# When the second weight-sum buffer of a gate/up pair is claimed: with the other three, or where it is first written

## The chip, the core and the metric

The kernel runs on one core of a Trainium2 chip. The core has a matrix engine (PE, with its weight loads as PEld), a vector engine (DVE), a scalar engine (ACT), a general engine (POOL) and a queue that issues transfers (SP). Each works through its own list of instructions in order and waits on semaphores of the others. The metric is the time of one execution in microseconds (us), as the median of several runs. A profiled execution gives the trace, in which times count from the first instruction.

## The reference

One layer of a hybrid block: a mixer of four parts, a cross attention over a memory, and a feed-forward part, each followed by a layer norm. The change lies in the feed-forward part:

```python
D_MODEL = 1024; SEQ = 1024; D_FF = 2816

def swiglu_ffn(x, w_gate, w_up, w_down):
    return (jax.nn.silu(x @ w_gate) * (x @ w_up)) @ w_down
...
        h = swiglu_ffn(x, w_ff_gate[l], w_ff_up[l], w_ff_down[l])
        x = layer_norm(DEEPNORM_ALPHA * x + h, ln_ff_g[l], ln_ff_b[l])
```

All arrays are float32.

## The kernel before

The 2816 columns of the gate and up weights are cut into 22 tiles of 128, taken two at a time: 11 pairs (`NPAIR`). For each pair the 2x2 blocks of weights and of x are multiplied by a scheme with seven block products in place of eight, so sums and differences of weight blocks are needed. A product is 24 matmuls of 128x512: two halves of the output (m = 0, 1), four blocks of depth, and three matmuls each, since every operand is split in a high and a low part (`whi`, `wlo`; `split`, L149 on ACT and L150 on DVE).

`gu_stream` (L622 to L658) makes the weights of the products, pair after pair, as a generator that is asked for a product two ahead of PE. For a pair it loads four tiles of 128x1024: `r11` and `r12` into `wraw` buffers, `r21` and `r22` into `gr` buffers (L627). POOL then makes s1 = r21 + r22, s2 = s1 - r11, r21 = r11 - r21 and r12 = r12 - s2 (all L631). s1 and s2 stand in two `gs` buffers, the last sum is written over the `wraw` of r12. The seven weights are used in the order r11, r12, s1, s2, r12', r21', r22.

`gu_first` runs the products of r11 and r12 into the banks `gc`; after the first, ACT copies the two halves of the bank to a buffer `ge` (L679), and the second accumulates into the same banks, so its halves wait for those copies. `gu_rest` runs the other five into `gb`, `ga`, `gb`, `ga`, `ga`; DVE takes the halves out (L694), and POOL makes four more sums of the results (L694), which SP stores (`hA`, `hS`, L713). From the third pair on, `down_sums` (L604 to L612) has POOL prepare one pair of rows of the down weights: two loads into `dw` buffers (L608), four differences (L611), four stores (`tT`, L612). The later down stage reads `hS` and `tT` again.

The 128x1024 buffers all come from one pool of 37, `c4`, and a scheduler that simulates the program decides at build time which freed buffer a claim gets, and how the instructions stand on each engine. A claim writes two columns on POOL at once, and is held in the order of all other claims, so that it waits on POOL until the buffer's last reader is done:

```python
    def big(self, s, dt=F32):
        t = self.c4.tile([P, 1024], dt, tag="c4", name=self.nm(s))
        i = self.nc.gpsimd.memset(t[:, 0:2].bitcast(F32), 0.0)
        if self.touch is not None:
            self.order(i, self.touch)
```

In the profile these claims are the MEMSET rows of L136. A load into a claimed buffer follows its claim.

Of the kernel before, what the change touches and what calls it, by code (L numbers as in the profile page):

```python
# [37 lines left out]
class Kernel:  # L38
# [583 lines left out]
    def gu_stream(self):  # L622
        nc, g = self.nc, self.nc.gpsimd
        wt = lambda: self.wp.tile([P, WCH], F32, tag="wraw", name=self.nm("wraw"), bufs=3)

        def load(t, i, q):
            nc.sync.dma_start(t, self.a["w_gu"][i, q])  # L627
            return t

        def sub(o, x, y, op=ALU.subtract):  # L630
            g.tensor_tensor(out=o, in0=x, in1=y, op=op)  # L631

        for i in range(NFIRST):
            for q in range(2):
                yield self.versions(load(wt(), i, q))
        for i in range(NPAIR):
            r11 = load(wt(), i, 0)
            if i >= NFIRST:
                yield self.versions(r11)
            r12 = load(wt(), i, 1)  # L640
            t = self.g0 if i == 0 else [self.big(n) for n in ("gr", "gr", "gs", "gs")]
            r21, r22, s1, s2 = load(t[0], i, 2), load(t[1], i, 3), t[2], t[3]
            sub(s1, r21, r22, ALU.add)
            if i >= NFIRST:
                yield self.versions(r12)
            sub(s2, s1, r11)
            yield self.versions(s1)
            sub(r21, r11, r21)
            sub(r12, r12, s2)
            yield self.versions(s2)  # L650
            yield self.versions(r12)
            yield self.versions(r21)
            yield self.versions(r22)
# [1170 lines left out]
```

## Time and profile before

| | |
|---|---|
| median of 3 runs | 1496.89 us (1494.80 to 1496.94) |
| profiled execution | 1496.83 us, span of its instructions 1495.0 us |
| PE busy | 1437.6 us (96%) |
| DVE, ACT, POOL busy | 937.3, 521.8, 330.5 us |
| mean granted TensorE clock | 0.984 of full speed |

The profiled execution is within 0.1 us of the median of the runs. A busy PE row counts matmuls that run one behind another; time in which PE waits shows as idle before a row, with what ended it in square brackets. Gate and up take from about 806 to 1268 us of the span, the down products from there to 1484 us.

### The profile page before, as it was taken

Reading aid. Unit: us, or ns where it says so; the run is one execution under the profiler, and the core shown is the slowest. Engines: PE = TensorE matmul, PEld = TensorE weight load, DVE = VectorE, ACT = ScalarE, POOL = GpSimd, SP = SyncE. Lnnn points to the kernel's source line nnn. Section 1 sums busy time; section 2 is a strip of 40 time slices with the busy share of each in tenths; the row PEclk is TensorE's granted clock in tenths of the full one; section 3 lists DMA queues with packets and bytes.
Section 4 is the critical chain, followed back from the end, with each engine's and each line's share of the span. In section 5 each row is a group of like instructions: output and inputs, shape, how many; then the busy total and the mean of one; then the engine's idle time right before and its main releaser. Section 6 shows DMA issues by size and latency. Waiting matters only on the chain.

```text
span 1495.0 us, 20717 instructions
## 1 busy us (share of the span) xinstructions
PE 1437.6 (96%) x7778; PEld 1174.6 (79%) x7778; DVE 937.3 (63%) x1622; ACT 521.8 (35%) x828; POOL 330.5 (22%) x598
## 2 busy tenths in 40 slices
PE   8799999999999999999999899999999998999996
PEld 6687787778788888888888777878877786888885
DVE  7968545485567388557549967645555455555557
ACT  4214533342245033443335522222222223433324
POOL 6300000010000000000010557656555540000003
PEclk9899999999999999999999999999999999999999
DMA  6532011010438103115214244444444457666612
GB/s 221 155 88 97 29 64 36 29 43 2 143 111 308 67 29 99 57 64 175 72 43 155 85 134 169 162 156 154 162 162 140 132 177 282 210 193 198 187 45 107
DMA packets 71508, 184.70 MB, mean 124 GB/s; under 512 B 8544, under 2 KB 9328, under 8 KB 71408
## 3 DMA queue, kind: packets, MB, share of 16 engines
q1 hardware_dynamic: 69680, 180.23, 36.3%
q10 hardware_dynamic: 1728, 3.15, 0.6%
q8 instruction: 61, 1.00, 0.3%
q14 instruction: 39, 0.32, 0.1%
HBM read 141.79 MB, written 41.55 MB: 123 GB/s over the span
## 4 chain that ended last, share of the span: by engine, by line
PE 63%; DMA 12%; POOL 11%; DVE 7%; issue 4%; ACT 1%; SPq 1%; POOLq 0%; DVEq 0%; ACTq 0%
PE fm L73 8%; PE da L73 7%; PE q L73 6%; PE wo L73 5%; PE mx L73 5%; PE dr L73 5%; DMA gr<-in_w_gu 3%; DMA dw<-in_w_down 3%; PE dn L73 3%; POOL dw L611 3%; POOL gs L631 2%; PE gc L73 2%; PE ds L73 2%; PE ga L73 2%; POOL gr L631 2%
## 5 line engine op out<-in xcount | busy, mean ns | idle before, releaser
L150 DVE TENSOR_TENSOR wlo<-wraw,whi 128x1024 fp32r<-128x1024 f32 (+3 forms) x177 | 233.8, 1323 | 141.8 <-ACT whi L149 141.1
L149 ACT CAST whi<-wraw 128x1024 fp32r<-128x1024 f32 (+3 forms) x177 | 183.3, 1038 | 300.5 <-PE da L73 58.5
L73 PE MATMUL ga<-xv,whi 128*128 128x512 f32 x528 | 164.9, 394 | 10.6 <-DVE gq L694 10.5
L73 PE MATMUL gc<-xv,whi 128*128 128x512 f32 x352 | 113.9, 406 | 13.9 <-ACT ge L679 13.8
L73 PEld LDWEIGHTS ga<-xv,whi 128*128 128x128 f32 x528 | 100.0, 190 | 33.1 <-issue 12.2
L73 PE MATMUL gb<-xv,whi 128*128 128x512 f32 x352 | 108.6, 390 | 0.0
L73 PE MATMUL ga<-xv,wlo 128*128 128x512 f32 x264 | 103.7, 393 | 0.0
L73 PEld LDWEIGHTS gc<-xv,whi 128*128 128x128 f32 x352 | 67.9, 195 | 30.6 <-ACT ge L679 16.4
L73 PE MATMUL fm<-xh,whi 128*128 128x512 f32 x208 | 86.0, 414 | 0.0
L73 PE MATMUL wo<-whi,oT 128*128 128x512 f32 x256 | 82.1, 394 | 0.0
L73 PE MATMUL fm<-xh,wlo 128*128 128x512 f32 x208 | 81.5, 392 | 0.0
L73 PE MATMUL fm<-xl,whi 128*128 128x512 f32 x208 | 81.3, 391 | 0.0
L73 PE MATMUL mx<-whi,yT 128*128 128x512 f32 x256 | 80.6, 392 | 0.4 <-DVE X L355 0.3
L73 PEld LDWEIGHTS gb<-xv,whi 128*128 128x128 f32 x352 | 66.4, 189 | 13.9
L73 PE MATMUL gc<-xv,wlo 128*128 128x512 f32 x176 | 70.5, 400 | 0.0
L73 PE MATMUL gb<-xv,wlo 128*128 128x512 f32 x176 | 68.5, 389 | 0.0
L263 POOL TENSOR_TENSOR X<-X,ln_ff_b 128x1024 f32<-128x1024 f32 x7 | 16.7, 2386 | 215.1 <-ACT X L262 215.1
L73 PEld LDWEIGHTS ga<-xv,wlo 128*128 128x128 f32 x264 | 50.1, 190 | 10.6
L73 PEld LDWEIGHTS mx<-whi,yT 128*128 128x128 f32 x256 | 48.1, 188 | 11.0 <-DVE X L355 0.7
L73 PE MATMUL da<-whi 128*128 128x512 f32 x144 | 56.2, 390 | 0.0
L73 PE MATMUL da<-wlo,whi 128*128 128x512 f32 x144 | 56.0, 389 | 0.0
L73 PE MATMUL da<-whi,wlo 128*128 128x512 f32 x144 | 56.0, 389 | 0.0
(500 smaller groups left out, 3324.9 us busy)
## 6 DMA issues: line engine op xcount, KB each, us to landing
wraw<-in_w_gu SPq DMA_DIRECT2D x28, 512.0 KB, 4.2
gr<-in_w_gu SPq DMA_DIRECT2D x22, 512.0 KB, 5.0
dw<-in_w_down SPq DMA_DIRECT2D x18, 512.0 KB, 3.6
tT<-dw SPq DMA_DIRECT2D x36, 256.0 KB, 2.2
wraw<-hS SPq DMA_DIRECT2D x36, 256.0 KB, 2.7
wraw<-tT SPq DMA_DIRECT2D x36, 256.0 KB, 3.1
wraw<-in_w_q SPq DMA_DIRECT2D x16, 512.0 KB, 4.2
wraw<-in_w_o SPq DMA_DIRECT2D x16, 512.0 KB, 3.5
```

The costliest lines, as they stand in the source:

```text
L73: return self.pin(self.nc.tensor.matmul(*a, **k))
L149: return (self.nc.scalar.copy(out=hi, in_=src), self.nc.vector.tensor_tensor(out=lo, in0=src, in1=hi.bitcast(F32), op=ALU.subtract))
L150: self.nc.vector.tensor_tensor(out=lo, in0=src, in1=hi.bitcast(F32), op=ALU.subtract))
L263: nc.gpsimd.tensor_tensor(out=x, in0=x, in1=b, op=ALU.add)
L611: nc.gpsimd.tensor_tensor(out=o, in0=x, in1=y, op=ALU.subtract)
L631: g.tensor_tensor(out=o, in0=x, in1=y, op=op)
```

## The change

The claims of a pair were made at one place, all four together, before the first sum. Now r21, r22 and s1 are claimed where they are first needed, which is still the same place, and s2 is claimed just ahead of the instruction that writes it, which from the fourth pair on comes after the generator has paused for the product of r12. The first pair keeps its four buffers, which were claimed earlier. The sums, the loads and the products are the same.

```diff
@@ -638,11 +638,13 @@
             if i >= NFIRST:
                 yield self.versions(r11)
             r12 = load(wt(), i, 1)
-            t = self.g0 if i == 0 else [self.big(n) for n in ("gr", "gr", "gs", "gs")]
-            r21, r22, s1, s2 = load(t[0], i, 2), load(t[1], i, 3), t[2], t[3]
+            new = (lambda n: self.g0.pop(0)) if i == 0 else self.big
+            r21, r22 = load(new("gr"), i, 2), load(new("gr"), i, 3)
+            s1 = new("gs")
             sub(s1, r21, r22, ALU.add)
             if i >= NFIRST:
                 yield self.versions(r12)
+            s2 = new("gs")
             sub(s2, s1, r11)
             yield self.versions(s1)
             sub(r21, r11, r21)
```

The lists of PE, DVE and ACT hold the same operations in the same order. Those of POOL and SP change in the last eight of the eleven pairs, seven of them alike. On POOL, in one of these pairs before (two claims of `gs`: s1, then s2; `dw` are the down weights, `ge` the buffer of the next pair's copies):

```order
L136 MEMSET gs_9045 128x2
L631 TENSOR_TENSOR gs_9045<-gr_9041,gr_9043 128x1024
L136 MEMSET gs_9047 128x2
L631 TENSOR_TENSOR gr_9041<-wraw_8996,gr_9041 128x1024
L631 TENSOR_TENSOR gs_9047<-gs_9045,wraw_8996 128x1024
L136 MEMSET dw_9087 128x2
L611 TENSOR_TENSOR dw_9087<-dw_9087 128x512
L136 MEMSET dw_9089 128x2
L611 TENSOR_TENSOR dw_9087<-dw_9089,dw_9087 128x512
L611 TENSOR_TENSOR dw_9089<-dw_9089,dw_9087 128x512
L611 TENSOR_TENSOR dw_9089<-dw_9089 128x512
L136 MEMSET ge_9101 128x2
```

On POOL at the same place now:

```order
L136 MEMSET gs_9047 128x2
L631 TENSOR_TENSOR gs_9047<-gr_9041,gr_9044 128x1024
L136 MEMSET dw_9085 128x2
L631 TENSOR_TENSOR gr_9041<-wraw_8996,gr_9041 128x1024
L611 TENSOR_TENSOR dw_9085<-dw_9085 128x512
L136 MEMSET dw_9087 128x2
L611 TENSOR_TENSOR dw_9085<-dw_9087,dw_9085 128x512
L611 TENSOR_TENSOR dw_9087<-dw_9087,dw_9085 128x512
L136 MEMSET ge_9099 128x2
L611 TENSOR_TENSOR dw_9087<-dw_9087 128x512
L136 MEMSET gs_9104 128x2
L631 TENSOR_TENSOR gs_9104<-gs_9047,wraw_8996 128x1024
```

The first `dw` claim has moved up behind s1, and s2 with its claim has moved down behind all four differences of the down weights. In both lists a claim of `gq`, the result sum into `gu` (L694), the weight sum into `wraw` (L631) and the further result sums follow. The claims pass the freed buffers on in the same succession, so each gets another one: the first `dw` now takes the buffer that s2 had (freed by the stores of `ge`), and s2 takes the one that `ge` had (freed by the stores of the first `dw`).

On SP at the same place, before (stores of `ge`, the load of the next pair's r11, loads of `dw`, stores `tT` of the differences, the load of the next pair's r12):

```order
L713 DMA hA_113<-ge_8555 128x512
L713 DMA hS_118<-ge_8555 128x512
L627 DMA wraw_9269<-in_w_gu 128x1024
L713 DMA hA_119<-h_8832 128x512
L608 DMA dw_9087<-in_w_down 128x1024
L612 DMA tT_174<-dw_9087 128x512
L608 DMA dw_9089<-in_w_down 128x1024
L612 DMA tT_176<-dw_9087 128x512
L627 DMA wraw_9312<-in_w_gu 128x1024
L612 DMA tT_175<-dw_9089 128x512
L612 DMA tT_177<-dw_9089 128x512
```

On SP now:

```order
L715 DMA hA_113<-ge_8553 128x512
L715 DMA hS_118<-ge_8553 128x512
L608 DMA dw_9085<-in_w_down 128x1024
L627 DMA wraw_9269<-in_w_gu 128x1024
L612 DMA tT_174<-dw_9085 128x512
L715 DMA hA_119<-h_8830 128x512
L608 DMA dw_9087<-in_w_down 128x1024
L612 DMA tT_176<-dw_9085 128x512
L612 DMA tT_175<-dw_9087 128x512
L612 DMA tT_177<-dw_9087 128x512
L627 DMA wraw_9312<-in_w_gu 128x1024
```

The first `dw` load now stands ahead of the load of r11, and the load of r12 behind all the stores of the differences; it waits for s2, which reads the `wraw` buffer it refills.

## Rows read from the trace of the kernel before

**Rows 1.** Timeline of PE, gate and up: start, duration, operation, idle time before it, releaser.

```profile
935.29 0.70 PE L73 MATMUL ga<-xv,whi 128*128 128x512 f32 x2 [1.77 <-DVE gq L694]
990.36 1.22 PE L73 MATMUL gc<-xv,whi 128*128 128x512 f32 x2 [3.14 <-ACT ge L679]
1110.05 0.73 PE L73 MATMUL gc<-xv,whi 128*128 128x512 f32 x2 [2.41 <-ACT ge L679]
1149.84 0.73 PE L73 MATMUL gc<-xv,whi 128*128 128x512 f32 x2 [1.42 <-ACT ge L679]
1190.86 1.22 PE L73 MATMUL gc<-xv,whi 128*128 128x512 f32 x2 [2.65 <-ACT ge L679]
1260.46 1.19 PE L73 MATMUL ga<-xv,whi 128*128 128x512 f32 x2 [5.12 <-DVE gq L694]
```

**Rows 2.** The chain that ended last: start, duration, what.

```profile
1190.86 4.51 PE gc L73 x12
1195.37 5.45 PE gb L73 x24
...
1260.46 8.19 PE ga L73 x24
```

**Rows 3.** Windows: length, busy time by engine, granted clock, DMA share, GB/s.

```profile
990.30:995.70 5.40, 5.34 (x13) 4.23 (x14) 0.78 (x1) 0.70 (x3) 3.33 (x5) 0.50 0.64 174
```

**Rows 4.** Timeline of ACT at the stall of 1110 us.

```profile
1099.37 1.06 ACT L149 CAST whi<-gs 128x1024 fp32r<-128x1024 f32 x1 [1.21 <-PE ga L73]
1102.28 0.59 ACT L679 COPY ge<-gc 128x512 f32<-128x512 f32 x1 [1.86 <-PE gc L73]
1108.46 1.05 ACT L149 CAST whi<-wraw 128x1024 fp32r<-128x1024 f32 x1 [5.60 <-POOL wraw L631]
```

**Rows 5.** Timeline of POOL ahead of the stall of 1110 us.

```profile
1077.79 2.40 POOL L631 TENSOR_TENSOR gs<-gr,gr 128x1024 f32<-128x1024 f32 x1 [5.32 <-DMA gr<-in_w_gu]
...
1080.26 3.27 POOL L631 TENSOR_TENSOR gr<-wraw,gr 128x1024 f32<-128x1024 f32 x1
1083.50 2.39 POOL L631 TENSOR_TENSOR gs<-gs,wraw 128x1024 f32<-128x1024 f32 x1
...
1089.60 1.68 POOL L611 TENSOR_TENSOR dw<-dw 128x512 f32<-128x512 f32 x1 [3.67 <-DMA dw<-in_w_down]
...
1095.68 3.54 POOL L611 TENSOR_TENSOR dw<-dw,dw 128x512 f32<-128x512 f32 x2 [4.37 <-DMA dw<-in_w_down]
1099.30 1.30 POOL L611 TENSOR_TENSOR dw<-dw 128x512 f32<-128x512 f32 x1
...
1104.75 0.10 POOL L136 MEMSET gq<- 128x2 f32 x1 [4.11 <-DMA tT<-dw]
...
1106.06 2.38 POOL L631 TENSOR_TENSOR wraw<-wraw,gs 128x1024 f32<-128x1024 f32 x1
...
1118.35 2.40 POOL L631 TENSOR_TENSOR gs<-gr,gr 128x1024 f32<-128x1024 f32 x1 [4.97 <-DMA gr<-in_w_gu]
```

**Rows 6.** Timeline of SP at the same place.

```profile
1085.95 0.33 SPq L608 DMA_DIRECT2D dw<-in_w_down  x1
1091.72 0.38 SPq L608 DMA_DIRECT2D dw<-in_w_down  x1
```

**Rows 7.** The page: transfers by line, issues, KB each, us to landing.

```profile
gr<-in_w_gu SPq DMA_DIRECT2D x22, 512.0 KB, 5.0
...
tT<-dw SPq DMA_DIRECT2D x36, 256.0 KB, 2.2
```

**Rows 8.** Timeline of DVE and POOL ahead of the stall of 935 us.

```profile
931.14 3.41 DVE L150 TENSOR_TENSOR wlo<-wraw,whi 128x1024 fp32r<-128x1024 f32 x1
934.47 1.28 DVE L694 TENSOR_TENSOR gq<-ga,gq 128x512 f32<-128x512 f32 x2
...
930.62 2.84 POOL L631 TENSOR_TENSOR gr<-wraw,gr 128x1024 f32<-128x1024 f32 x1
```

**Rows 9.** Timelines of DVE, POOL and ACT ahead of the stall of 1260 us.

```profile
1218.62 2.30 DVE L150 TENSOR_TENSOR wlo<-gs,whi 128x1024 fp32r<-128x1024 f32 x1
...
1227.48 0.18 POOL L136 MEMSET X<- 128x2 f32 x3
...
1249.33 1.05 ACT L149 CAST dv<-dr 128x1024 fp32r<-128x1024 f32 x1 [9.51 <-DMA dr<-hA]
```

## The prediction

> **What bounds the kernel now.** The table of the profile has PE busy for 96% of the span, so only time in which PE waits, or runs at its lower clock, can be won. I looked first for PE's waits in gate and up [rows 1]: from 935 us on there are six, 16.5 us together. Four have one cause: the second product of a pair (into `gc`) waits for ACT's copy to `ge`, 3.14 + 2.41 + 1.42 + 2.65 = 9.62 us. The other two wait for DVE: 1.77 us at 935 and 5.12 us at 1260.
>
> A wait can cost more than itself. After the one at 990 us the granted clock stood at 0.50, the level of 1.2 GHz, for 5.4 us [rows 3], which is 2.7 us of work at the level of 2.4 GHz: 2.7 us lost. After the one at 1191 us twelve matmuls took 4.51 us, where 24 take 5.45 [rows 2], so 4.51 - 2.73 = 1.8 us lost. After 1260 us 24 matmuls took 8.19 us, 2.74 us lost. After the other two `gc` waits the first two matmuls took 0.73 us, as good as nothing lost.
>
> Why does ACT copy late? On ACT [rows 4] the cast of the `wraw` sum waited 5.60 us for POOL and ended at 1109.51; the copy of the second half of `gc` stands behind it, and PE went on at 1110.05. So the chain of POOL is what is late. Follow it from the end of s1 at 1080.19 [rows 5]: r21, s2, then 3.67 us of waiting for the first `dw`, one difference, 4.37 us for the second `dw`, three differences, 4.11 us until a store of `dw` has landed and frees the buffer that `gq` claims, the result sum into `gu`, and the `wraw` sum, which ends at 1108.44. That is 28.25 us. The next s1 ends at 1120.75, so the whole turn of POOL took 40.56 us. PE needs seven products of 5.45 us for a pair, 38.15 us. POOL is the slower of the two here, and PE waits when it has used up its lead.
>
> **The change, part by part.** It adds and removes no instruction: 8 claims of s2 and 8 sums of s2 move, and with them two transfers of each pair. The stalls inside POOL's chain are what it touches. I count from the end of s1, with the durations of [rows 5].
>
> 1. The first `dw` is claimed at once, and its load is issued at about 0.25 (0.12 after the claim, as at 1085.95 [rows 6] behind the claim before it). It used to run against nothing: 3.65 us from its issue to the difference at 1089.60. Now r21 (3.27 us) covers it, but the load of the next pair's r11 is issued right behind it. Lower bound 0.25 + 3.65 = 3.9; upper bound from two loads of 512 KB side by side, the `gr` pair, 5.0 us to landing [rows 7], 5.2. I take the middle: the difference starts at 4.5 and ends, 1.68 us long, at 6.2.
> 2. The second `dw` load was issued 0.44 us after that end [rows 5, 6]; one store (`hA`) now stands ahead of it, about 0.35 us more as such issues take [rows 6]: issue at 7.0, and 3.96 us later (1091.72 to 1095.68) the next two differences: 11.0 to 14.5. The last one ends at 15.9.
> 3. s2's claim waits for the stores of the first `dw`, the later of them issued at about 12.8. Such a store takes 2.2 us [rows 7], up to the 4.15 us that `gq`'s claim needed behind the last difference: no wait, at most 1.1 us. I take none. s2 ends at 18.4.
> 4. The claim of `gq` still waits for the last store, 4.15 us after 15.9, so at 20.05; s2 has filled that wait instead of standing ahead of it. The result sum and the `wraw` sum follow as before (1104.75 to 1108.44, 3.69 us) and end at 23.7.
>
> So 28.25 becomes 23.7, 4.5 us less (with the lower bounds of all steps some 7, with the upper ones 2.8). The turn is then 40.56 - 4.5 = 36.0 us, under PE's 38.15: PE sets the pace, and POOL's lag shrinks by some 2 us a pair. The four `gc` waits go: 9.62 us and the clock's 2.7 + 1.8, together **14.1 us**.
>
> What moves late: s2 ended 5.7 us after s1 and now ends at 18.4. Its cast on ACT began at 1099.37, 19.2 after s1 [rows 4], and is therefore just met. Behind it stands the copy of the first half of `gc`, at 1102.28, with 1.85 us of room. The load of the next r12, which now also waits for s2, was issued behind the second difference before, at about 17.5 (1095.68 and half of 3.54 us), so it all but keeps its place, and it has the next pair's start to land. The `h` store and the stores of differences are read in the down stage only.
>
> What moves early is not free either. DVE and POOL get in each other's way: the split `wlo` at 931.14 took 3.41 us, of which only 1.09 lie behind the end of POOL's r21 (933.46), and the take-out of `gq` behind it came 1.77 us late for PE [rows 1, 8]. The tight place is the stretch from 16.4 to 21.8 us (three to four products) after a pair's first `gb` matmul: there the two `ga` products follow each other in the same banks. In the pair of [rows 5] it lies at about 1089 to 1094 us (the half product that stalled was due at 1107.6, six and a half products or 35.4 us after the first `gb` matmul), where POOL did one difference and waited for the second `dw`. As its lag shrinks, s2 passes through it. I allow one new stall of that kind, **-1.8 us**, and leave the old one at 935 as it is.
>
> The Trainium skill, page "SBUF — State Buffer", section "SBUF: two separate sides", says that DVE, with two operands from SBUF, and GpSimd take a shared pair of ports by an exclusive lock that is held for the whole instruction. The trace agrees (the two ends 1.09 us apart). Taken alone, the rule speaks against the change, because it lets POOL work in place of a wait; the sum by it is that of the first rival.
>
> The last stall, at 1260 us, is of another make: ACT waited 9.51 us for `dr` [rows 9], in a queue of transfers behind eight loads of X, which begin once POOL has claimed their buffers at 1227.48. The first of these buffers was free at 1220.92, after DVE's split. With POOL's chain 4.5 us shorter the loads start about that much sooner against PE. The stall's 5.12 + 2.74 = 7.9 us bound what is to be had; nothing is had if `dr` is held by PE's own products. I take **4 us**.
>
> Sum: 14.1 - 1.8 + 4 = 16.3 us off the profiled execution's 1496.8 us, which is as good as the median: 1480.5 us.
>
> **The rivals.**
> - *DVE is blocked in every pair.* If POOL, now almost never waiting, holds up the splits in the tight stretch in all seven later pairs at 1.77 us each, 12.4 us are given back: 1496.8 - 14.1 - 4 + 12.4 = 1491; with four such pairs 1486. For it: the stall at 935 came just so. Against it: once the lag is gone, the `gu` and `wraw` sums wait for DVE themselves, so only s2 can be in the way.
> - *The wait only moves.* Each claim still waits for somebody's store. If the first `dw` lands as late behind the load of r11, and s2's claim waits for its stores, by 4.5 us together, the chain is as long as before: 1497. Against it: the steps above would all have to pass their upper bounds.
> - *s2 becomes the late weight: slower.* It decides if s2 ends later than 19.2 + 1.85 + 2.1 = 23.2 after s1 (the cast's start, the room ahead of the copy, and half a product of 2.73 us less the copy's 0.59), 4.8 us later than worked out. Then ACT holds the copy back in each of eight pairs; at 2.65 us each, the largest of the later waits, that is 21.2 us in place of the 14.1 removed: 1504.
> - *The end gives all.* The whole 7.9 us at 1260 us and the 1.8 us allowed for go too: 1496.8 - 14.1 - 7.9 = 1475, less the old stall at 935, 1473.
>
> **How the numbers follow.** Forecast 0.55 (1476 to 1486), blocked DVE 0.20, moved wait 0.08, slower 0.09, all of the end 0.08. The range 1474 to 1491 takes in the forecast, most of the first rival and of the last. A change of 0.2%, 3 us, is about what a measurement of this kernel can tell from none: faster 0.84, same 0.07, slower 0.09.
>
> **What would show it.** Right: on POOL, the wait ahead of the first `dw` difference about 1 us and not 3.67, s2 between the last difference and the claim of `gq`, that claim's wait under 2 us, and a turn from s1 to s1 of 38 us, with the wait now ahead of the `gu` sum, for DVE; on PE no `gc` wait for ACT after 935 us. Wrong: waits of `ga` for DVE in many pairs (first rival), `dw` or s2's claim waiting 4 us or more (second), ACT's cast of `gs` waiting for POOL (third). The end is right if ACT's wait for `dr` falls to about 5 us.

## The result, and the profile after

The changed kernel took 1476.44 us (median of 4 runs, 1470.48 to 1478.25), the kernel before beside it 1496.91 (4 runs, 1494.8 to 1499.27): a ratio of 0.9856, interval 0.9824 to 0.9887; the medians are 20.5 us apart. In a second comparison (`e_after_again` below) the ratio was 0.9879, interval 0.9855 to 0.9902, which is 18 us less (15 to 22). The profiled execution of after took 1470.48 us. Line numbers of after are those of before, two higher behind the edit (L696 for L694, L681 for L679).

The first part of the page, after (busy time, share of the span, instructions):

```profile
PE 1428.1 (97%) x7778; PEld 1167.7 (80%) x7778; DVE 938.7 (64%) x1622; ACT 522.0 (36%) x828; POOL 340.8 (23%) x598
```

The waits of PE in the stretch from 900 to 1300 us, first of before (whose single rows are [rows 1]), then of after: total, times, longest.

```profile
PE gc L73 <- ACT ge L679: 9.6, 4, 3.1
PE ga L73 <- DVE gq L694: 6.9, 2, 5.1
```

```profile
PE ga L73 <- DVE gq L696: 0.5, 1, 0.5
```

All four `gc` waits are gone, the stall of 1260 us too, and that of 935 us is 0.53 us long: 16.0 us of waiting. With the low clock that the prediction counted behind them (2.7 + 1.8 + 2.74) this is 23.2 us. The two profiled executions are 26.3 us apart. Of the rest, 2.8 us lie ahead of anything that the change touches: on PE's timeline the last transposes of x start at 810.92 us before and at 808.10 after. So some 3 us of that distance are not the change's. The execution profiled is also the fastest of the four, so the sum of 23.2 us belongs to these two executions, and the runs show 18 to 20.5 us.

Now POOL, one turn of after, the stretch that answers to [rows 5]:

```profile
1025.89 2.39 POOL L631 TENSOR_TENSOR gs<-gr,gr 128x1024 f32<-128x1024 f32 x1 [5.33 <-DMA gr<-in_w_gu]
...
1032.56 1.30 POOL L611 TENSOR_TENSOR dw<-dw 128x512 f32<-128x512 f32 x1 [0.93 <-DMA dw<-in_w_down]
...
1039.51 2.67 POOL L611 TENSOR_TENSOR dw<-dw,dw 128x512 f32<-128x512 f32 x2 [5.61 <-DMA dw<-in_w_down]
...
1042.26 1.82 POOL L611 TENSOR_TENSOR dw<-dw 128x512 f32<-128x512 f32 x1
...
1044.20 3.23 POOL L631 TENSOR_TENSOR gs<-gs,wraw 128x1024 f32<-128x1024 f32 x1
1047.38 0.09 POOL L136 MEMSET gq<- 128x2 f32 x1
...
1048.68 2.86 POOL L631 TENSOR_TENSOR wraw<-wraw,gs 128x1024 f32<-128x1024 f32 x1
...
1061.42 2.40 POOL L631 TENSOR_TENSOR gs<-gr,gr 128x1024 f32<-128x1024 f32 x1 [3.39 <-DMA gr<-in_w_gu]
```

The wait ahead of the first `dw` difference is 0.93 us where [rows 5] has 3.67, s2 stands behind the last difference, and the claim of `gq`, which waited 4.11 us, waits for nothing. The turn is 35.53 us against 40.56. Over the seven turns of the later pairs the waits of POOL add up as follows, before (from 950 to 1225 us) and after (950 to 1200 us):

```profile
POOL dw L611 <- DMA dw<-in_w_down: 55.7, 14, 4.4
POOL gs L631 <- DMA gr<-in_w_gu: 38.9, 7, 7.5
POOL gq L136 <- DMA tT<-dw: 22.9, 7, 4.9
```

```profile
POOL dw L611 <- DMA dw<-in_w_down: 41.2, 14, 5.6
POOL gs L631 <- DMA gr<-in_w_gu: 25.5, 7, 5.5
POOL wraw L631 <- DVE wlo L150: 3.6, 1, 3.6
POOL gu L696 <- DVE gu L696: 3.6, 3, 1.8
```

The waits of `gq`'s claim for stores go entirely and those for `dw` shrink. Small waits of other claims for stores come in (4.3 us in all), and waits for DVE in the last three turns, which is POOL having caught up with PE.

### The profile page after: what moved, and what is told of

Same layout as the page of the kernel before. It is cut to its first block, busy times and chain, and to the rows that moved or that the text cites. A ratio compares the mean times of both kernels' runs of the same rounds, so it can differ in the third digit from the quotient of the medians.

```text
span 1468.7 us, 20723 instructions
## 1 busy us (share of the span) xinstructions
PE 1428.1 (97%) x7778; PEld 1167.7 (80%) x7778; DVE 938.7 (64%) x1622; ACT 522.0 (36%) x828; POOL 340.8 (23%) x598
## 4 chain that ended last, share of the span: by engine, by line
PE 85%; DVE 8%; DMA 3%; issue 2%; ACT 1%; POOL 1%; SPq 0%; DVEq 0%; POOLq 0%; ACTq 0%
PE ga L73 11%; PE fm L73 8%; PE gb L73 7%; PE gc L73 7%; PE da L73 7%; PE q L73 6%; PE wo L73 6%; PE mx L73 5%; PE dr L73 5%; PE dn L73 3%; PE ds L73 2%; PE gv L73 2%; PE s L73 2%; DVE wlo L150 2%; PE pv L73 1%
## 5 line engine op out<-in xcount | busy, mean ns | idle before, releaser
L150 DVE TENSOR_TENSOR wlo<-wraw,whi 128x1024 fp32r<-128x1024 f32 (+3 forms) x177 | 230.2, 1303 | 126.1 <-ACT whi L149 125.2
L73 PE MATMUL gc<-xv,whi 128*128 128x512 f32 x352 | 110.7, 396 | 5.1 <-ACT ge L681 5.0
L73 PEld LDWEIGHTS ga<-xv,wlo 128*128 128x128 f32 x264 | 49.6, 188 | 10.3
```

The source lines that it names most:

```text
L73: return self.pin(self.nc.tensor.matmul(*a, **k))
L150: self.nc.vector.tensor_tensor(out=lo, in0=src, in1=hi.bitcast(F32), op=ALU.subtract))
```

## The experiments

All ratios are to the kernel before on the same chip, whose median lay between 1492.5 and 1498.5 us there. The times in the expectations count from about 1497 us for the kernel before, so I hold them against the ratio.

**`e_after_again`: the changed kernel once more.**

> The changed kernel once more, for a closer interval and a second trace. If the first trace (span 1468.7 us) shows the rule, the median is 1470 to 1473 us and its trace again has no wait of PE after 935 us. If the first trace was a lucky one, the median is 1476 to 1479 us and the trace has either a wait ahead of the last pair's products, as the 5.12 us before, or one or two waits of ga for DVE of about 1.8 us, as the first rival has it.

1473.34 us, 0.9879, interval 0.9855 to 0.9902. The only wait of PE behind 934 us is the small one of `ga` for DVE. The gain repeats.

**`e_not_last` and `e_last`: the late claim in all pairs but the last, and in the last alone.** The edit to the changed kernel, here for `e_last` (`e_not_last` has `i < NPAIR - 1`):

```diff
             s1 = new("gs")
+            late = i == NPAIR - 1
+            if not late:
+                s2 = new("gs")
             sub(s1, r21, r22, ALU.add)
             if i >= NFIRST:
                 yield self.versions(r12)
-            s2 = new("gs")
+            if late:
+                s2 = new("gs")
```

> The late claim in all pairs but the last; the last pair claims its buffers together, as before. If the stall of 5.12 us ahead of the last products went because POOL no longer lags behind PE, it stays away: the same as the full change within 2 us. If it went because of the last pair's own order on POOL and SP, it comes back with 5 to 8 us, and the time is 1482 to 1485 us.

> The late claim in the last pair alone; all others claim together, as before. The four waits of gc for ACT stay (14 us). If POOL's lag makes the last stall, the last pair's chain, 4.5 us shorter, takes away about 4.5 us of it and some of the low clock behind it: 1489 to 1493 us. If the last pair's own order makes it, all 7.9 us go: 1489 us. If neither, 1497 us.

`e_not_last`: 1474.57 us, 0.9885, interval 0.9861 to 0.9909, as the full change. `e_last`: 1490.75 us, 0.9997, interval 0.9982 to 1.0013. The last stall is 0.81 us long in `e_not_last`, at 1247.72 us, and 5.13 us in `e_last`, at 1259.51.

So the last pair's own order gives nothing, and the 4.5 us that the first theory let its shorter chain take off the stall did not come either. The stall is made by what POOL's chain has lost in the pairs ahead of it, and goes with that.

**`e_dw_ahead`: the claims of s1 and s2 side by side again, the first `dw` claimed and loaded between them.** s2 is summed ahead of the second `dw`, so its claim is not late, only the load is early. The core of the edit to the changed kernel:

```diff
-            r21, r22 = load(new("gr"), i, 2), load(new("gr"), i, 3)
-            s1 = new("gs")
+            r21, r22, s1 = load(new("gr"), i, 2), load(new("gr"), i, 3), new("gs")
+            if i >= NFIRST:
+                self.dw[i - 2] = self.down_load(i - 2)
+            s2 = new("gs")
             sub(s1, r21, r22, ALU.add)
...
-            s2 = new("gs")
```

> As before the change, but the first down-weight buffer of a pair is claimed and its load issued between the claims of s1 and s2; s2 keeps its place ahead of the last three differences. From s1's end: first difference to 6.2, s2 to 8.6, second load issued 8.7, differences 12.7 to 17.6, claim of gq 21.8, wraw sum to 25.4, so 2.85 us less than the 28.25 before, a turn of 37.7 us against PE's 38.15: if overlapping the load is what counts, nearly the whole gain, 1477 to 1483 us. If what counts is that s2 fills the wait for the stores, it gives little: 1490 to 1497 us.

1474.61 us, 0.9885, interval 0.9861 to 0.9909: nearly the whole gain, as the first theory had it. POOL in `e_dw_ahead`:

```profile
1035.07 1.29 POOL L614 TENSOR_TENSOR dw<-dw 128x512 f32<-128x512 f32 x1 [1.20 <-DMA dw<-in_w_down]
...
1036.48 2.40 POOL L634 TENSOR_TENSOR gs<-gs,wraw 128x1024 f32<-128x1024 f32 x1
...
1042.44 2.67 POOL L614 TENSOR_TENSOR dw<-dw,dw 128x512 f32<-128x512 f32 x2 [3.52 <-DMA dw<-in_w_down]
...
1049.58 0.10 POOL L136 MEMSET gq<- 128x2 f32 x1 [2.74 <-DMA tT<-dw]
```

s2 fills a part of the second `dw`'s wait here (3.52 us where after has 5.61), and the `gq` claim waits 2.74 us. The sum of the turn is the same (35.2 us from 1029.00 to 1064.22), and so is the time. Of these two places it doesn't matter in which s2 stands: in both it fills a wait, and the first load is early.

**`e_sum_late`: all claims as before, s2's sum alone behind the four `dw` differences.** So s2 fills the wait ahead of `gq`'s claim, while the `dw` loads stay late. The core of the edit to the kernel before, in which `t4` is the last difference:

```diff
-            sub(s2, s1, r11)
+            late = sub(s2, s1, r11)
+            if i >= NFIRST:
+                self.order(late, self.t4)
```

> As before the change, all four buffers claimed together, but the sum s2 itself ordered behind the four differences of the down weights. From s1's end: r21 to 3.3, the first dw load issued 3.5, difference 7.1 to 8.8, second load 9.3, differences 13.2 to 18.1, s2 to 20.5, claim of gq 22.2, wraw sum 25.9 instead of 28.25: a turn of 38.2 us, level with PE's 38.15. If POOL's turn is the cause, nearly the whole gain, with one short wait or none: 1474 to 1482 us. If the early load of dw is what counts, nothing: 1490 to 1495 us.

1483.97 us, 0.9913, interval 0.9888 to 0.9938: 13 us of the gain (9 to 17), 2 us short of the first theory's range and 6 us from the second's. The turns took 37.6 to 38.7 us, level with PE's 38.15. Of the `gc` waits behind 935 us one of 1.15 us is left, but the last stall is back at its full size. PE and ACT of `e_sum_late`:

```profile
1248.29 1.19 PE L73 MATMUL ga<-xv,whi 128*128 128x512 f32 x2 [5.11 <-DVE gq L696]
...
1237.17 1.05 ACT L149 CAST dv<-dr 128x1024 fp32r<-128x1024 f32 x1 [10.38 <-DMA dr<-hA]
```

This parts the two halves of the gain. A turn as short as PE's ends the `gc` waits; only a shorter one lets POOL catch up, and then the last stall goes too. That the early load alone takes it away is ruled out by `e_after_twice`, next, which keeps that load and has the stall again.

**`e_before_twice`, `e_after_twice`, `e_after_thrice`: s2's sum made two or three times in the later pairs.** Each repetition writes the same values again. The edit, here for two:

```diff
-            sub(s2, s1, r11)
+            for _ in range(2 if i >= NFIRST else 1):
+                sub(s2, s1, r11)
```

> As before the change, but the sum s2 is done twice in each of the eight pairs, 2.4 us more on POOL, the result the same. If POOL's turn sets the pace, its turn becomes 43 us, and the time grows by some 2.4 us a pair: 16 to 20 us, 1508 to 1513 us. If POOL's wait for transfers is what it is and takes up added work, 0 to 5 us more.

> As after the change, with the sum s2 done twice in the same pairs. If POOL's turn counts, it becomes 38.4 to 39 us, 0.3 to 0.8 us over PE's: the lag does not shrink, and the end pays: 3 to 9 us over the changed kernel, 1476 to 1482 us. If the changed order had merely hidden POOL, nothing: 1473 us. If DVE is blocked by POOL's work in the tight stretch (the first rival), waits of ga for DVE of 1 to 2 us in most pairs and 10 us or more.

> As after the change, with the sum s2 done three times in the same pairs: a turn of 40.8 to 41.5 us, that of before. If the length of POOL's turn is all that matters and not the order, the whole gain is gone: 1492 to 1500 us, with waits of gc for ACT of 2 to 3 us a pair and the stall ahead of the last products back. If the order itself matters, it stays under 1485 us.

`e_before_twice`: 1515.02 us, 1.0116, interval 1.0087 to 1.0145: 17 us more than before, as expected. `e_after_twice`: 1490.26 us, 0.9957, interval 0.9942 to 0.9972; that is 0.8 to 1.0% over the changed kernel's two ratios, 12 to 15 us, where 3 to 9 were expected. `e_after_thrice`: 1507.99 us, 1.0089, interval 1.0064 to 1.0113, slower than before, and above what either theory allowed. PE's waits from 806 to 1290 us in `e_after_twice`:

```profile
PE gc L73 <- ACT ge L682: 9.6, 8, 5.3
PE ga L73 <- DVE gq L697: 7.3, 3, 3.6
PE ga L73 <- DVE gu L697: 4.5, 1, 4.5
```

Doubled, the turn of after is 38.2 to 40.1 us. One `gc` wait of 5.3 us and one of `ga`, 3.6 us, lie ahead of 900 us, where after has such waits too (5.03 and 3.29 us). The other seven `gc` waits are worth 4.3 us (seven, of 18.0 us, in `e_before_twice`), so the miss lies at the end: two stalls, of 4.46 and 3.55 us, come back there with their low clock. Between 900 and 1240 us `ga` waits for DVE once, for 0.16 us, though POOL works 2.4 us more in each pair; that speaks against the first rival. Tripled, the third rival's mechanism appears. ACT of `e_after_thrice`:

```profile
1073.62 1.04 ACT L149 CAST whi<-gs 128x1024 fp32r<-128x1024 f32 x1 [3.84 <-POOL gs L631]
1074.57 0.58 ACT L682 COPY ge<-gc 128x512 f32<-128x512 f32 x1
1078.21 1.04 ACT L149 CAST whi<-wraw 128x1024 fp32r<-128x1024 f32 x1 [3.07 <-POOL wraw L631]
1079.16 0.58 ACT L682 COPY ge<-gc 128x512 f32<-128x512 f32 x1
```

The cast of s2 now waits for POOL, and the first copy stands behind it, so that PE waits twice in most pairs. s2 ended there at 1073.59, 24.3 us after the end of s1 (1046.86 + 2.40 = 1049.26), beyond the 23.2 us from which that rival was to decide. But POOL's turn is longer here too (41.2 us on average between 966 and 1213 us, against 40.3 before and 41.8 in `e_before_twice`, which took 17 us more with s2 early), so this run doesn't show how much of its 13 us over before the late s2 is worth.

**`e_x_late`, `e_x_late6`, `e_before_x4`: are the loads of X what holds up the last stall's `dr`?** In all runs with the stall, X was claimed late. In `e_x_late` and `e_x_late6` loads of X in the changed kernel also wait for ACT's cast of r21 in the last pair; `e_x_late6` has

```diff
-            nc.sync.dma_start(self.X[t], self.xdr[t])
+            ld = nc.sync.dma_start(self.X[t], self.xdr[t])
+            if t >= 2:
+                self.gate(ld, self.late_x)
```

(`e_x_late` has `t == 3`), and `e_before_x4` is the kernel before with only four loads of X ahead of the first `dr`:

```diff
+        load_x((4, 5, 6, 7))
...
+        last(NST, NST, 1)
+        load_x((0, 1, 2, 3))
         product(ac, True, lambda j: (X[j], hs[0], ALPHA))
-        last(NST, NST, 1)
```

> The changed kernel, in which the fourth load of X also waits until ACT has cast r21 of the last pair, so that five of the eight loads of X run as late against PE as in the kernel before; nothing else is moved. Theory, the loads of X hold up the first dr and with it the last stall: the gc waits stay away, but a stall of 4 to 5.1 us of ga for DVE is back in the last pair, with some 2.7 us of low clock, so 6 to 8 us over the changed kernel: 1480 to 1485, ratio 0.990 to 0.992. Rival, POOL's lag itself makes that stall and the loads of X only go along with it: 1473 to 1478, ratio under 0.988, and no stall over 1 us behind 1240 us.

> The changed kernel, in which six of the eight loads of X wait until ACT has cast r21 of the last pair and so stand right ahead of the first dr loads on SP; POOL's claims and chain stay as changed, and PE's order too. Theory, the transfers of X ahead of dr make the last stall: ACT's wait for the first dr goes from 3.5 back to 8 us or more, and ga for DVE stalls 3 to 6 us in the last pair, 4 to 8 us over the changed kernel, ratio 0.988 to 0.992. Rival, the stall needs POOL's lag (its late claims of dv and dr) and not the loads of X: no stall over 1 us behind 1230 us, ratio under 0.988.

> The kernel before, with four loads of X ahead of the first dr loads and the other four behind them, in place of eight ahead; the claims of s1 and s2 and POOL's chain are untouched. Theory, the loads of X hold up the first dr: ACT's wait for it falls from 9.5 to under 6 us, the last stall of 5.1 us goes to under 1 us, the four gc waits stay as they are: 6 to 8 us less than before, 1487 to 1491, ratio 0.994 to 0.996. Rival, POOL's lag itself makes the stall: within 2 us of the kernel before, with the stall still at 5 us.

`e_x_late`: 1472.56 us, 0.9859, interval 0.9834 to 0.9883. The other loads passed the one that waits, so a single load was late, and the run says nothing on the question. `e_x_late6`: 1473.48 us, 0.9832, interval 0.9810 to 0.9855, no stall. `e_before_x4`: 1492.25 us, 0.9993, interval 0.9974 to 1.0011, with the stall at 2.64 us. SP, then ACT, of `e_x_late6`:

```profile
1219.54 3.02 SPq L777 DMA_DIRECT2D X<-xdr  x6
1222.66 0.98 SPq L801 DMA_DIRECT2D dr<-hA  x2
...
1223.61 1.06 ACT L149 CAST whi<-gr 128x1024 fp32r<-128x1024 f32 x1 [4.38 <-DMA X<-xdr]
1229.01 1.05 ACT L149 CAST whi<-wraw 128x1024 fp32r<-128x1024 f32 x1 [4.34 <-PE ga L73]
1232.18 1.05 ACT L149 CAST dv<-dr 128x1024 fp32r<-128x1024 f32 x1 [2.12 <-DMA dr<-hA]
```

Six loads stand right ahead of `dr`, and `dr` comes late: 9.5 us from the issue to the cast. But the scheduler put the cast of `dr` behind that of `wraw` this time, and it holds nobody up. In `e_before_x4` it went the other way: `dr` was cast 9.0 us after r21 (1232.12 to 1241.08) where before it was 16.0 (1233.33 to 1249.33), but the cast was put ahead of that of r22. In this profile the stall is 2.5 us shorter and the granted clock behind it 1.00 in place of 0.50, some 5 us in all; the runs show 1 us less, at most 4. PE and ACT there:

```profile
1256.65 0.70 PE L73 MATMUL ga<-xv,whi 128*128 128x512 f32 x2 [2.64 <-DVE gq L694]
...
1241.08 1.05 ACT L149 CAST dv<-dr 128x1024 fp32r<-128x1024 f32 x1 [7.91 <-DMA dr<-hA]
...
1243.40 1.05 ACT L149 CAST whi<-gr 128x1024 fp32r<-128x1024 f32 x1
```

So the expectation missed in both, and the theory as I put it falls: late loads of X alone don't make the stall. It takes a late `dr` and its split standing ahead of the take-outs in the queues of ACT and DVE. With the order of these queues left alone, late loads of X were not tried.

**`e_both_ahead`: both `dw` buffers claimed and loaded between s1 and s2**, as in `e_dw_ahead` but for both loads:

```diff
+            if i >= NFIRST:
+                self.dw[i - 2] = [self.down_load(f) for f in (i - 2, i - 2 + NPAIR)]
+            s2 = new("gs")
             sub(s1, r21, r22, ALU.add)
```

> Both dw buffers are claimed and their loads issued between the claims of s1 and s2, so that the second dw wait of 4.7 to 5.6 us goes from POOL's chain as well. Theory, after the change PE sets the pace and POOL has time to spare: within 3 us of the changed kernel, ratio 0.984 to 0.988, and POOL's time is spent waiting for DVE ahead of the gu and wraw sums. Rival, POOL's chain still counts, as PE still waits some us early in gate and up: 4 us or more faster than the changed kernel, ratio under 0.983. Slower if the two loads side by side hold up r21 or r22 of the next pair, or DVE is blocked: over 0.990, with waits of ga for DVE.

1473.39 us, 0.9876, interval 0.9853 to 0.9899: the time of the changed kernel. But the edit did not do what it was for. POOL of `e_both_ahead`:

```profile
1034.04 0.10 POOL L136 MEMSET dw<- 128x2 f32 x1
1040.04 2.65 POOL L614 TENSOR_TENSOR dw<-dw,dw 128x512 f32<-128x512 f32 x2 [5.90 <-DMA dw<-in_w_down]
```

The second `dw` is still claimed behind the first difference (which ended at 1034.11), where the scheduler put it, and its wait stays (40.5 us over the seven turns for both loads, 41.2 in after). So an earlier second load was not tried. It could win little: PE waits 0.5 us between 900 and 1300 us in after. No version was faster than the changed kernel by more than the intervals allow.

## Why the prediction was right

**The chain of POOL: right, step by step.** From the end of s1 (1028.28) in the turn shown above, against the four steps: the first difference starts at 4.28 (4.5 predicted), the pair of differences at 11.23 (11.0), the last one ends at 15.8 (15.9), s2 ends at 19.15 (18.4), the claim of `gq` at 19.1 (20.05), the `wraw` sum ends at 23.3 (23.7). The turn is 35.5 (36.0); the first five behind 957 us take 35.4 to 36.6 us, and the sixth, with POOL caught up, 38.0, the figure that the prediction named as a sign. Two steps are off by amounts that cancel. The second `dw` wait is longer (5.61 us where 4.8 follow from the steps), and s2 took 3.23 us, but `gq`'s claim never waited.

s2's 3.23 us, where [rows 5] has 2.39, show the contention that the first rival spoke of. DVE in after, at the same time:

```profile
1042.85 2.31 DVE L150 TENSOR_TENSOR wlo<-wraw,whi 128x1024 fp32r<-128x1024 f32 x1
...
1046.89 0.69 DVE L696 TENSOR_TENSOR gq<-ga,gq 128x512 f32<-128x512 f32 x1 [1.12 <-PE ga L73]
```

The split, 1.22 us long where it stands alone, ends at 1045.16, 1.08 us behind the end of POOL's difference (1044.08), and s2 ends at 1047.43, 2.27 us behind the split. So each held the other once. By the rule of the Trainium skill that the prediction cites (page "SBUF — State Buffer", section "SBUF: two separate sides"), the later one is locked out for the whole instruction of the other; the trace agrees, since what is left of the split behind the difference, and of s2 behind the split, is about the length of each alone. But the half of `gq` at 1046.89 still had 1.12 us to wait for PE: DVE had that much to spare, and POOL had its lag to work off. Over the whole execution the same 598 instructions kept POOL busy for 340.8 us, 10.3 us longer than before. That this is the same holding up is likely and not shown row by row; it fell into time in which POOL had been waiting.

**14.1 us for the `gc` waits: right.** None is left behind 935 us. That they hang on POOL's turn against PE's 38.15 us is shown from both sides: 38 us (`e_sum_late`) all but ends them, 36 us (`e_dw_ahead`) ends them, and lengthening the turn brings them back in before and after alike (18.0 and 4.3 us, with s2 made twice). The 4.5 us of low clock in this term belong to the profiled execution of before: `e_last` and `e_before_x4`, with 7.1 and 10.1 us of `gc` waits behind 935 us, lost 1.7 us each (granted clock 0.68 over 5.4 us behind one of the waits, 1.00 behind the other large ones).

**-1.8 us allowed for a blocked DVE: nothing of it came.** Behind 935 us `ga` never waits for DVE in after, and the old wait at 935 us fell from 1.77 to 0.53 (0.73 in the second profile). Even with s2 made twice, no pair behind it shows what the first rival needs.

**4 us at the end: mis-sized, 7.9 came by the traces.** This term is most of what keeps the forecast 4 us above the median. By the two traces, the rival in which the end gives all is what happened: 14.1 + 7.9 + 1.2 = 23.2 us, 1473.6. The run times put it lower: `e_sum_late`, which keeps this stall, is 13 us faster than before and the changed kernel 18 to 20.5, so the end is worth 5 to 7.5 us, each figure uncertain by some 4 us. The forecast of 1480.5 lies just above what the first interval allows (0.9887 of 1496.9 is 1480.0) and inside the second (1475 to 1482), and the median of 1476.4 at the edge between the two cases. So the runs do not decide between them. By the traces the sum is 6.9 us short, by the runs only 2 to 4; that difference the prediction did not work out, and in that part its closeness is luck.

I took about half because I let the loads start earlier by the 4.5 us that POOL saves in one pair. But its lag was gathered over all pairs, and by the last one it is gone (`e_last` shows that the last pair's own saving is worth nothing). The row at 1227.48 [rows 9], from which I let the eight loads of X begin, has only three of their claims; the other five stand at 1234.28. DVE, POOL and SP of before, then POOL and SP of after:

```profile
1250.41 1.23 DVE L150 TENSOR_TENSOR dv<-dr,dv 128x1024 fp32r<-128x1024 f32 x1 [8.00 <-ACT dv L149]
1251.55 0.68 DVE L694 TENSOR_TENSOR gu<-ga,ge 128x512 f32<-128x512 f32 x1
...
1234.28 0.22 POOL L136 MEMSET X<- 128x2 f32 x5 [6.61 <-DMA hA<-ge]
1237.61 0.10 POOL L136 MEMSET dr<- 128x2 f32 x1
...
1229.14 7.70 SPq L773 DMA_DIRECT2D X<-xdr  x6
...
1239.63 0.33 SPq L713 DMA_DIRECT2D hA<-h  x1
1240.90 1.61 SPq L795 DMA_DIRECT2D dr<-hA  x2
```

```profile
1219.63 0.10 POOL L136 MEMSET dr<- 128x2 f32 x1
...
1207.52 4.36 SPq L775 DMA_DIRECT2D X<-xdr  x6
1219.60 0.81 SPq L797 DMA_DIRECT2D dr<-hA  x2
```

Before, the take-out of `gu` stands on DVE behind the split of `dr`, and that waits 8.00 us. The last five claims of X came late, so SP issued the last load of X only by 1236.84, and five more transfers stand between it and the load of `dr` in SP's order. To compare the two kernels, count from ACT's cast of r22 in the last pair, which waits only for PE (1238.76 before, 1220.78 after). The first claim of X comes at -11.3 before and at -18.9 after: 7.6 us earlier, and not 4.5. `dr` is claimed at -1.15 in both. SP issues its load at +2.14 before, behind that queue, and at -1.18 after, where it had issued nothing since 1216.63. It is cast at +10.57 before and +4.54 after: 3.3 us from the earlier issue, 2.7 from a shorter way (8.4 against 5.7 us), 6.0 together, which covers the stall of 5.1. Issue, cast and stall, for the twelve profiles in which ACT's cast of `dr` stands right behind that of r22:

```
                  dr issued   dr cast   stalls of ga
before              +2.14     +10.57    5.12
e_last              +2.37     +11.21    0.42 + 5.13
e_sum_late          +2.88     +11.43    0.64 + 5.11
e_after_twice       +6.47     +15.25    4.46 + 3.55
e_before_twice      +2.72     +11.27    0.50 + 5.15
e_after_thrice      +3.06     +11.70    0.91 + 5.14
e_dw_ahead          -1.19      +5.68    0.34
e_not_last          -1.18      +4.87    0.81
e_x_late            -1.19      +4.69    none
e_both_ahead        -1.18      +4.45    none
after               -1.18      +4.54    none
e_after_again       -1.19      +4.44    none
```

ACT's wait for `dr` in after is 3.48 us, under the 5 that the prediction named:

```profile
1225.32 1.05 ACT L149 CAST dv<-dr 128x1024 fp32r<-128x1024 f32 x1 [3.48 <-DMA dr<-hA]
```

The table and the queue orders of `e_x_late6` and `e_before_x4` fit one account: a late `dr`, cast in a fixed place of two in-order queues. How much of its lateness is SP's queue and how much the transfers ahead is read from the traces, and no run took the one away without the other.

**The other rivals.** The wait did not move: `dw` waits 0.2 to 1.4 us ahead of the first difference, and s2's claim once 1.3 us and else nothing. The slower case needs s2 at 23.2 us and has it at 19.15; `e_after_thrice`, with 24.3, shows the mechanism at work beyond that value and in a kernel slower than before, but not how much of that is the late s2 and how much the longer turn.

## What to carry to other kernels

A claim that waits in a fixed order holds up every load that is claimed behind it, so look for loads that could be issued under work that already stands ahead of them; where the displaced work then lands matters little if it fills a wait. Compare the turn of a helper engine with that of the engine that it feeds: once it is shorter, the waits go, and what is saved beyond that is not lost but catches up with everything queued at the end of the stage, so price the end with the lag that has gone, not with one turn's saving.

## What was not expected of the hardware

The length of a wait does not tell whether PE comes back at its lower clock. In the same place of the program, behind a `gc` wait at 990 us, the granted clock was 0.50 in before ([rows 3], a wait of 3.14 us, 2.7 us lost) and 1.00, the level of 2.4 GHz, in `e_before_x4`, behind a wait of 3.29 us. The wait and the window behind it, of `e_before_x4`:

```profile
990.85 0.73 PE L73 MATMUL gc<-xv,whi 128*128 128x512 f32 x2 [3.29 <-ACT ge L679]
...
990.79:996.19 5.40, 5.34 (x23) 4.43 (x24) 2.69 (x3) 1.56 (x3) 3.36 (x5) 1.00 0.61 184
```

Nor does the first matmul tell. In `e_before_twice` the two matmuls behind a wait of 3.55 us took 0.73 us as well, but the clock fell within the product, to 0.68 over the window:

```profile
1032.11 0.73 PE L73 MATMUL gc<-xv,whi 128*128 128x512 f32 x2 [3.55 <-ACT ge L680]
...
1032.10:1037.50 5.40, 5.39 (x17) 4.28 (x18) 1.51 (x3) 1.50 (x2) 3.28 (x5) 0.68 0.61 175
```

So a price put on a single wait of some 3 us is uncertain by up to 2.7 us here, more than two of the prediction's three terms were off.
